# Feed-forward of a decoder layer: two-level matrix products by seven block products in place of eight, layer one then layer two

## The chip, the cores and the metric

The kernel runs on one core of a Trainium2 chip. The metric is the device time of that core in microseconds (us), from launch to end; three runs of the kernel before gave 1788.17, 1789.99 and 1790.69, median 1789.99.

The engines are called PE (matrix products), PEld (its weight loads), DVE (vector), ACT (scalar, activations), POOL (GpSimd) and SP (the queue that issues all loads and stores here).

## The reference

One layer of a decoder with 1024 tokens of width 1024 and a feed-forward width of 4096. Only the last part is touched by the change:

```python
y = jnp.einsum('bsk,kd->bsd', y_mix, w_out)              # output projection
x = layer_norm(DEEPNORM_ALPHA * x + (1.0 + g1) * y, ln1_g, ln1_b)
h = x * (1.0 + sc2) + sh2
ff = jnp.einsum('bsf,fd->bsd',
                jnp.square(jax.nn.relu(jnp.einsum('bsd,df->bsf', h, w_ff_in))),
                w_ff_out)
x = layer_norm(DEEPNORM_ALPHA * x + (1.0 + g2) * ff, ln2_g, ln2_b)
```

Ahead of it stand an input projection, a state-space scan and attention, which the change leaves as they are.

## The kernel before

All data are 32-bit floats. A product of two matrices is made from high and low parts: `hi` is the operand rounded to the matrix engine's format, `lo` the rest, and each product is three matmuls, hi·hi, hi·lo and lo·hi. Making the two parts is called a split here (`split`, lines 79 to 88): one cast for `hi` (ACT or POOL) and one subtraction on DVE for `lo` (line 85), which reads two tiles in SBUF.

The stages are, in order of time: modulation and input projection, scan, attention, then the output projection with the first LayerNorm (a loop over 8 blocks of 128 tokens, `tb`, lines 778 to 798), then the feed-forward (lines 800 to 900).

In the loop over `tb`, `norm` makes the normalized rows `u`, and `to_h2`, one block late, transposes them on PE (line 766, PSUM slots "S"), applies scale and bias on ACT (line 769) and splits the result into `h2` (ACT, DVE).

The feed-forward walks over 32 tiles `f` of 128 of the 4096 hidden columns. `ff1(f)` loads and splits a tile of `w1`, runs 48 matmuls of 512 columns (two token halves, 8 steps of k, 3 parts) and makes relu, square and split of the activations: ACT line 821, POOL line 822, ACT line 823, DVE line 824. `w2_prep(f)` loads a tile of `w2`, multiplies it by the gate row on POOL (line 831) and splits it. The activations never leave SBUF. Tiles are taken in groups (14 of two tiles, then one of four); per group the second layer runs over the 8 token blocks, and each result, 1024 columns in one PSUM slot "S", is added to the block's accumulator `ffacc` by DVE (line 883; ACT line 881 in the first group). POOL adds the residual at some point between (lines 876 to 878). In the last group each block goes straight from its matmuls to the second LayerNorm (`norm`, lines 739 to 748), two more row operations (lines 898, 899) and the store.

The kernel is written against a tile framework: tags name rings of buffers (`SLOTS`), a scheduler orders each engine's instructions, and each engine then runs its own list strictly in order. All DMAs stand in one list, SP's.

Of the kernel before, what the change touches and what calls it, by code (L numbers as in the profile page):

```python
# [32 lines left out]
def layer_kernel(ctx, tc, x, xT, cols, rows3, w_ada, b_ada, w_in, w_dtf, w_out, ln_rows, w1, w2, out):  # L33
# [767 lines left out]
    acctags = ["pt"] * 4 + ["P"] * 3 + ["cum"]  # L801
    acc = [None] * TB
    with after(marks["y", 1, 7]):
        g2row = mod_row(G2, "cum", "g2row")

    def ff1(f):
        with after(marks["y", 1, 7]):
            w, _ = w_prep(w1[f], tag=("w", "P")[f % 2])
        ahi = R4("qk", "a_hi")
        alo = R4("qk", "a_lo")  # L810
        for half in range(2):
            hs = slice(half * 512, half * 512 + 512)
            o = PT(("mm", "t", "o", "t")[(2 * f + half) % 4], "mm_ps")
            for k in range(KT):
                xhi, xlo = (t[:, k % 4, :] for t in h2[half][k // 4])
                whi, wlo = wk_(w, k)
                mm(o, whi, xhi, k == 0, False)
                mm(o, whi, xlo, False, False)
                mm(o, wlo, xhi, False, k == KT - 1)
            r = sm.tile([P, 512], F32, name="ffr", tag="o_half", bufs=2)  # L820
            nc.scalar.activation(r, o, AF.Relu)  # L821
            nc.gpsimd.tensor_tensor(r, r, r, op=ALU.mult)  # L822
            nc.scalar.copy(ahi[:, hs], r)  # L823
            nc.vector.tensor_tensor(alo[:, hs], r, ahi[:, hs].bitcast(F32), op=ALU.subtract)  # L824
        return ahi, alo

    def w2_prep(f, tag):
        raw = T4("raw", "raw_w2")
        with after(marks["y", 1, 7]):
            load(raw, w2[f * P:(f + 1) * P, :])  # L830
        nc.gpsimd.tensor_tensor(raw, raw, g2row, op=ALU.mult)  # L831
        hi = R4(tag, "w2_hi")
        lo = R4(tag, "w2_lo")
        split(raw, hi, lo, "act")
        return hi, lo

    groups = [2] * 14 + [4]
    f = 0
    for gi, gf in enumerate(groups):
        final = gi == len(groups) - 1  # L840
        a = []
        w = []
        for i in range(gf):
            a.append(ff1(f))
            w.append(w2_prep(f, "v" if i < 2 else "misc" if i == 2 else "w"))
            f += 1
        if final:
            with after(marks["y", 1, 7]):
                ln2g = row(2, "hx", "ln2g")
                ln2b = row(3, "hx", "ln2b")  # L850
        for tb in range(TB):
            ts = slice(tb * P, (tb + 1) * P)
            last = final and tb == TB - 1
            if last:
                oh = [PT("S", "s_ps"), PT("S", "s_ps")]
            else:
                o = PT("S", "s_ps", (P, 1024))
                oh = [o[:, :512], o[:, 512:]]
            for half in range(2):
                ds = slice(half * 512, half * 512 + 512)  # L860
                for i in range(gf):
                    mm(oh[half], a[i][0][:, ts], w[i][0][:, ds], i == 0, False)
                    mm(oh[half], a[i][0][:, ts], w[i][1][:, ds], False, False)
                    mm(oh[half], a[i][1][:, ts], w[i][0][:, ds], False, i == gf - 1)
            u = acc[tb]
            if gi == 1 and tb == 0:
                with after(marks["y", 1, 7]):
                    ln1g = row(0, "misc", "ln1g")
                    ln1b = row(1, "misc", "ln1b")
                nc.gpsimd.tensor_scalar(ln1g, ln1g, ALPHA, 1.0, op0=ALU.mult, op1=ALU.mult)  # L870
                nc.gpsimd.tensor_scalar(ln1b, ln1b, ALPHA, 1.0, op0=ALU.mult, op1=ALU.mult)
            if gi == tb + 1:
# [85 lines left out]
```

## Time and profile before

| | |
|---|---|
| median of three runs | 1789.99 us (1788.17 to 1790.69) |
| profiled execution: span | 1789.5 us |
| mean granted PE clock over the span | 0.988 |
| PE busy | 1731.2 us, 97% |
| DVE busy | 1136.4 us, 64% |
| POOL busy | 731.2 us, 41% |
| ACT busy | 607.2 us, 34% |

The profiled execution's span is 1789.5 us; its three timed siblings have their median 0.5 us above that. A busy share is the time in which an engine executes something; PE at 97% has very little time in which it waits. The feed-forward is the stretch from about 1070 us to the end.

### The profile page before, as it was taken

To read this page: it belongs to the slowest core of one execution; us is meant where nothing else is said; L and a number is where in the kernel's file an instruction comes from. 1 tells how busy PE (TensorE), PEld (TensorE's weight loads), DVE (VectorE), ACT (ScalarE), POOL (GpSimd) and SP (SyncE) were. 2 spreads that over 40 slices of the span, in tenths; PEclk is the share of its full clock that TensorE was granted. 3 is DMA by queue.
4 is the path that set the end of the run, shared out by engine and by line. 5 is a ranking of instruction groups with operands and counts; after the bars stand their busy time and mean duration, and the time that the engine had idled before them with its cause. 6 is when DMAs were issued, how large, how long until landed. Compare 5 with 4: busy or idle time off the path is not lost.

```text
span 1789.5 us, 22841 instructions
## 1 busy us (share of the span) xinstructions
PE 1731.2 (97%) x8676; PEld 1441.7 (81%) x8676; DVE 1136.4 (64%) x1771; ACT 607.2 (34%) x1035; POOL 731.2 (41%) x634
## 2 busy tenths in 40 slices
PE   7989999999999999999999999999999999999996
PEld 6768888888888888887788887888888888888885
DVE  7778687768777777757664774354554544455448
ACT  3445333314444545446654443211111111111121
POOL 5143344335445444424423547444444432223235
PEclk9989999999999999999999999999999999999998
DMA  8134334322233232223237442211111111111112
GB/s 322 36 131 132 114 133 138 110 71 82 83 117 102 93 115 89 64 62 127 97 129 235 136 175 102 71 60 59 48 59 59 59 47 48 47 48 47 48 71 94
DMA packets 73117, 172.76 MB, mean 97 GB/s; under 512 B 7696, under 2 KB 34576, under 8 KB 73008
## 3 DMA queue, kind: packets, MB, share of 16 engines
q1 hardware_dynamic: 73008, 171.31, 28.4%
q8 instruction: 68, 1.11, 0.3%
q14 instruction: 41, 0.34, 0.1%
HBM read 140.74 MB, written 22.15 MB: 91 GB/s over the span
## 4 chain that ended last, share of the span: by engine, by line
PE 75%; DVE 12%; DMA 4%; ACT 3%; issue 3%; POOL 3%; SPq 0%; DVEq 0%; POOLq 0%; ACTq 0%
PE mm_ps L62 45%; PE s_ps L62 22%; PE o_ps L62 4%; PE t_ps L523 3%; DVE ada_red L134 2%; DMA raw_ada<-in_w_ada_dram 1%; DVE conv_a L326 1%; DVE scores L398 1%; DVE w_hl L85 1%; DVE scores L396 1%; DVE probs L496 1%; DMA raw_o<-in_w_out_dram 1%; DVE h_hl L85 1%; DVE ffacc L898 0%; DVE pt_hl L526 0%
## 5 line engine op out<-in xcount | busy, mean ns | idle before, releaser
L62 PE MATMUL mm_ps<-h_hl,w_hl 128*128 128x512 f32 x3552 | 865.8, 396 | 6.0 <-DVE w_hl L85 4.6
L62 PEld LDWEIGHTS mm_ps<-h_hl,w_hl 128*128 128x128 f32 x3552 | 660.3, 189 | 142.2 <-DVE w_hl L85 7.0
L883 DVE TENSOR_TENSOR ffacc<-ffacc,s_ps 128x1024 f32<-128x1024 f32 x104 | 126.1, 1220 | 187.5 <-PE s_ps L62 187.5
L85 DVE TENSOR_TENSOR w_hl<-raw_w,w_hl 128x512 fp32r<-128x512 f32 x152 | 141.8, 949 | 99.2 <-POOL w_hl L79 99.0
L62 PE MATMUL s_ps<-w_hi,a_hi 128*128 128x512 f32 x512 | 199.9, 390 | 2.2 <-DVE ffacc L739 2.2
L62 PE MATMUL s_ps<-w_lo,a_hi 128*128 128x512 f32 x512 | 199.8, 390 | 0.0
L62 PE MATMUL s_ps<-w_hi,a_lo 128*128 128x512 f32 x512 | 198.2, 391 | 0.1
L79 POOL TENSOR_SCALAR w_hl<-raw_w 128x512 fp32r<-128x512 f32 x150 | 103.8, 701 | 188.8 <-PE mm_ps L62 85.6
L501 POOL TENSOR_SCALAR probs<-probs,m 128x128 f32<-128x128 f32 (+7 forms) x128 | 102.4, 803 | 155.9 <-DVE m L500 134.8
L822 POOL TENSOR_TENSOR ffr<-ffr 128x512 f32<-128x512 f32 x64 | 80.4, 1257 | 203.4 <-ACT ffr L821 203.3
L132 POOL TENSOR_TENSOR raw_ada<-raw_ada,c_act 128x1024 f32<-128x1024 f32 x44 | 90.1, 2055 | 117.3 <-DMA raw_ada<-in_w_ada_dram 95.9
L499 ACT ACTIVATE probs<-probs,m 128x128 f32<-128x128 f32 (+7 forms) x128 | 99.2, 776 | 91.0 <-DVE m L498 77.3
L821 ACT ACTIVATE ffr<-mm_ps 128x512 f32<-128x512 f32 x64 | 38.2, 597 | 268.6 <-PE mm_ps L62 265.3
L824 DVE TENSOR_TENSOR a_lo<-ffr,a_hi 128x512 fp32r<-128x512 f32 x64 | 65.1, 1017 | 93.2 <-ACT a_hi L823 90.7
L496 DVE CUSTOM_DVE_ANT_0 probs<-s_ps,cumrow 128x128 f32<-128x128 f32 (+7 forms) x128 | 95.1, 753 | 36.3 <-PE s_ps L62 23.0
L62 PEld LDWEIGHTS s_ps<-w_hi,a_hi 128*128 128x128 f32 x512 | 96.5, 189 | 22.8 <-DVE ffacc L739 2.7
L62 PE MATMUL o_ps<-pt_hl,v_s 128*128 128x256 f32 (+1 forms) x640 | 110.6, 294 | 3.6 <-DVE m L498 1.5
L525 ACT CAST pt_hl<-t_ps 128x512 fp32r<-128x512 f32 (+1 forms) x160 | 84.5, 541 | 86.5 <-PE t_ps L523 83.9
L62 PEld LDWEIGHTS s_ps<-w_hi,a_lo 128*128 128x128 f32 x512 | 96.4, 188 | 20.6 <-DVE a_lo L824 0.6
L526 DVE TENSOR_TENSOR pt_hl<-t_ps,pt_hl 128x512 fp32r<-128x512 f32 (+1 forms) x160 | 99.8, 633 | 20.4 <-ACT pt_hl L525 19.1
L62 PEld LDWEIGHTS s_ps<-w_lo,a_hi 128*128 128x128 f32 x512 | 96.5, 188 | 20.1
L831 POOL TENSOR_TENSOR raw_w<-raw_w,g2row 128x1024 f32<-128x1024 f32 x32 | 81.2, 2538 | 70.5 <-DMA raw_w<-in_w_dram 67.4
(209 smaller groups left out, 2557.1 us busy)
## 6 DMA issues: line engine op xcount, KB each, us to landing
raw_w<-in_w_dram SPq DMA_DIRECT2D x64, 512.0 KB, 3.3
raw_ada<-in_w_ada_dram SPq DMA_DIRECT2D x48, 512.0 KB, 3.8
raw_w<-in_w_in_dram SPq DMA_DIRECT2D x44, 512.0 KB, 3.6
arow<-rowd SPq DMA_DIRECT2D x16, 512.0 KB, 4.0
cumrow<-rowd SPq DMA_DIRECT2D x16, 512.0 KB, 3.6
q<-q_st SPq DMA_DIRECT2D x128, 64.0 KB, 2.0
y_raw<-yd SPq DMA_DIRECT2D x16, 512.0 KB, 4.5
raw_o<-in_w_out_dram SPq DMA_DIRECT2D x16, 512.0 KB, 3.4
```

What stands on the lines that cost most here:

```text
L62: nc.tensor.matmul(o, l, r, start=start, stop=stop)
L79: nc.gpsimd.tensor_scalar(hi, raw, 1.0, 1.0, op0=ALU.mult, op1=ALU.mult)
L85: eng.tensor_tensor(lo, raw, hi.bitcast(F32), op=ALU.subtract)
L132: nc.gpsimd.tensor_tensor(raw, raw, c_act.unsqueeze(2).broadcast_to([P, KT, P]), op=ALU.mult)
L496: nc.vector.tensor_tensor_reduce(out=pt, in0=sp[:, :W], in1=cum[:, :W], op0=ALU.add, op1=ALU.max, scale=1.0, scalar=-3.0e38, accum_out=m[: ...
L499: nc.scalar.activation(pt, pt, AF.Exp, bias=m[:, 1:2], scale=1.0, accum_out=m[:, 2:3])
L501: nc.gpsimd.tensor_scalar(pt, pt, m[:, 3:4], 1.0, op0=ALU.mult, op1=ALU.mult)
L525: nc.scalar.copy(hl[:, 0, :n], tp[:, :n])
L526: nc.vector.tensor_tensor(hl[:, 1, :n], tp[:, :n], hl[:, 0, :n].bitcast(F32), op=ALU.subtract)
L822: nc.gpsimd.tensor_tensor(r, r, r, op=ALU.mult)
L831: nc.gpsimd.tensor_tensor(raw, raw, g2row, op=ALU.mult)
L883: nc.vector.tensor_tensor(u, u, o, op=ALU.add)
```

## The change

Both layers of the feed-forward are computed by Strassen's scheme in Winograd's form: each matrix is cut into 2 by 2 blocks, sums and differences of blocks are formed first, seven block products are made in place of eight, and their sums give the four result blocks.

Layer 1 runs first for all hidden columns, in 16 `Pair`s of two `f` tiles. A pair is 7 products of 12 matmuls each (84 in place of 96). The operands on the side of `h2` are seven half-by-half matrices: three (numbers 1, 2, 3) are split in `to_h2`, four (5, 6, 4, 7) need differences between blocks of both token halves and are split by `h_split` behind the last block, as 16 tiles of 512 columns. On the weight side POOL makes four sums of 512 columns per pair, and ACT and DVE split all seven. Results are gathered in four PSUM banks X, Y, Z, V; even pairs take the banks "mm", "o", "t", "t", odd pairs the two slots "S". ACT copies four of them to SBUF, DVE adds three from PSUM and one from SBUF, and makes relu and square in one operation (four per pair, both inputs in SBUF). `out` stores the blocks and, after four more sums on POOL, the sums that layer 2 needs: seven tiles a pair, to DRAM.

Layer 2 covers 28 of the 32 tiles by Strassen, in seven "doubles" (groups of 2, 2, 2 and 1), and the last four tiles by plain products. Each double has seven products of 24 matmuls. Per product and double the activations come back from DRAM (512 KB), and both they and the `w2` sum (POOL) are split again. Each of the seven products has an accumulator `Q` of its own; ACT fills it in the first group, DVE adds to it in the others. In the last group DVE also makes the seven sums of 2048 columns that give the result blocks. POOL then multiplies by the gate row and adds the residual, 32 operations of 512 columns, and the last four tiles, the LayerNorm and the store follow per token block as before. The residual is now prepared during the first groups and kept in DRAM (`resd`).

Matmuls of 512 columns in the feed-forward: 1536 + 1536 before; 16·84 + 7·7·24 + 4·48 = 1344 + 1176 + 192 after.

The core of the diff:

```diff
+        if tb >= 4:
+            b12, b22 = hts
+            for i in range(2):
+                ks = slice(2 * i, 2 * i + 2)
+                t1, t4 = hf[0][:, ks, js], hf[1][:, ks, js]
+                sub(eng, t1, b12[:, ks, :], t1)
+                sub(eng, t3f[i][:, :, js], b22[:, ks, :], b12[:, ks, :])
+                sub(eng, t2f[i][:, :, js], b22[:, ks, :], t1)
+                sub(eng, t4, t4, t2f[i][:, :, js])
...
+    def h_split(o, src, tags):
+        hb_hl[o] = []
+        for k in range(4):
+            t = R4(tags[k], "h2_s", (P, 2, 512))
+            split(src(k), t[:, 0, :], t[:, 1, :], "act")
...
+    def w1_ops(n):
...
+        yield 1, op(a11)
+        yield 2, op(a12)
+        s3 = sm.tile([P, 4, P], F32, name="w_s3", tag="o_half", bufs=2)
+        sub(nc.gpsimd, s3, a11, a21)
+        add(nc.gpsimd, a21, a21, a22)
+        sub(nc.gpsimd, a11, a21, a11)
+        sub(nc.gpsimd, a12, a12, a11)
...
+        def run(self, steps):
...
+            def square(i):
+                nc.vector.scalar_tensor_tensor(c[:, i, :], c[:, i, :], 0.0, c[:, i, :], op0=ALU.max, op1=ALU.mult)
...
+                elif st == 7:
+                    self.product("X", False, True)
+                    nc.scalar.copy(u3, bank["X"])
+                    add(nc.vector, c[:, 1, :], bank["V"], u3)
+                    square(1)
+                    add(nc.vector, c[:, 2, :], p5, u3)
+                    square(2)
...
+    ORDER = (1, 2, 5, 6, 4, 7, 3)
+    first = [Pair(0), Pair(1)]
+    for p in first:
+        p.run(ORDER[:2])
+    h_split(5, lambda k: hf[0][:, k, :], ["qk"] * 4)
...
+    for gi, gd in enumerate(DOUBLES):
...
+                split(src, bhl[0], bhl[1], "act")
+                al_ = T4("v", "a_ld", shape=(P, 2, 512))
+                load(al_, adr[d][AD[i]])
+                ahl = [R4(t, "a_op", (P, 2, 512)) for t in atags]
+                split(al_, ahl[0], ahl[1], "act")
...
+                if gi == 0:
+                    nc.scalar.copy(q, o)
+                else:
+                    add(nc.vector, q, q, o)
+            if last:
+                if i == 2:
+                    add(nc.vector, Q[2], Q[2], Q[1])
...
+                elif i == 5:
+                    add(nc.vector, Q[3], Q[3], Q[6])
+                    add(nc.vector, Q[3], Q[3], Q[5])
+                    add(nc.vector, Q[5], Q[5], Q[7])
...
+        for h, u in enumerate(us):
+            ds = slice(h * 512, h * 512 + 512)
+            nc.gpsimd.tensor_tensor(u, u, g2row[:, ds], op=ALU.mult)
+            add(nc.gpsimd, u, u, rs[:, ds])
```

How the lists of the engines stand around two places. The first is the start of the feed-forward, where the last token block's rows `u` are transposed (`t_ps`). On PE before, the transposes are followed at once by the first layer's matmuls on operands that are already there:

```order
L766 MATMUL t_ps_9846<-identf_69,u1_9741 128x128 [waits Activation_49]
L766 MATMUL t_ps_9846<-identf_69,u1_9741 128x128 x3
L62 MATMUL mm_ps_9951<-h2_hl_8990,w_hl_9943 128x512 [waits Pool_49]
L62 MATMUL mm_ps_9951<-h2_hl_8991,w_hl_9943 128x512
L62 MATMUL mm_ps_9951<-h2_hl_8990,w_hl_9943 128x512 [waits DVE_49]
```

On PE now, one product of such operands (`h2_hl_8990`) is left, and behind it stands product 5 of the first pair, whose operands `h2_s_9997` and `w_op_10050` are made after the transposes; the matmuls on `h2_hl_8992` stand in the list behind that:

```order
L787 MATMUL t_ps_9880<-identf_69,u1_9769 128x128 x3
L911 MATMUL f_ps_9918<-h2_hl_8990,w_op_9964 128x512 [waits Activation_49]
L911 MATMUL f_ps_9918<-h2_hl_8990,w_op_9964 128x512 x5
L911 MATMUL f_ps_9918<-h2_hl_8991,w_op_9964 128x512 x6
L911 MATMUL f_ps_9913<-h2_s_9997,w_op_10050 128x512 [waits Activation_49]
L911 MATMUL f_ps_9913<-h2_s_9997,w_op_10050 128x512 [waits DVE_49]
...
L911 MATMUL f_ps_9914<-h2_s_10030,w_op_10082 128x512
L911 MATMUL f_ps_9918<-h2_hl_8992,w_op_9980 128x512 [waits Activation_49]
```

On ACT at the same place, these are the rows ahead of the cast of `w_op_10050` (the last eleven of 20 casts that stand between the last transposed block's activations and it):

```order
L81 CAST h2_s_10009<-h2_t2_8998 128x512 [waits DVE_49]
L81 CAST h2_s_10012<-h2_t2_8998 128x512
L81 CAST h2_s_10039<-h2_t3_9001 128x512 [waits DVE_49]
L81 CAST h2_s_10042<-h2_t3_9001 128x512
L81 CAST h2_s_10015<-h2_t2_8999 128x512 [waits DVE_49]
L81 CAST h2_s_10018<-h2_t2_8999 128x512
L81 CAST h2_s_10021<-h2_f_8997 128x512 [waits DVE_49,Pool_49]
L81 CAST h2_s_10024<-h2_f_8997 128x512
L81 CAST w_op_10082<-raw_w_9925 128x512 [waits DMAHW5_49]
L81 CAST h2_s_10027<-h2_f_8997 128x512 [waits DVE_49,Pool_49]
L81 CAST h2_s_10030<-h2_f_8997 128x512
L81 CAST w_op_10050<-raw_w_9925 128x512 [waits Pool_49]
```

Before, ACT had two casts there (`h2_hl_8994`, `h2_hl_8996`) and one of a weight.

The second place is the last group of layer 2. On DVE before, rows of this kind, one for each 12 matmuls of 512 columns, stood ahead of the last group, and the last group's own blocks went to the LayerNorm:

```order
L883 TENSOR_TENSOR ffacc_10106<-ffacc_10106,s_ps_13600 128x1024 [waits DVE_49,PE_49]
L824 TENSOR_TENSOR a_lo_13651<-ffr_13707,a_hi_13650 128x512 [waits Activation_49]
L883 TENSOR_TENSOR ffacc_10121<-ffacc_10121,s_ps_13614 128x1024 [waits DVE_49,PE_49]
L883 TENSOR_TENSOR ffacc_10136<-ffacc_10136,s_ps_13628 128x1024 [waits DVE_49,PE_49]
L85 TENSOR_TENSOR w2_lo_13716<-raw_w2_13712,w2_hi_13715 128x1024 [waits DVE_49,Activation_49]
```

On DVE now, the end of the last group (`q_acc_12387` is Q2, `12314` Q3, `12466` Q6, `12539` Q7, `12612` Q5, `12687` Q4); a row of 2048 columns is a sum of two accumulators, and those of one accumulator and `s_ps` free a PSUM slot:

```order
L765 TENSOR_TENSOR q_acc_12539<-q_acc_12539,q_acc_12466 128x2048 [waits DVE_49]
L765 TENSOR_TENSOR q_acc_12612<-q_acc_12612,s_ps_14066 128x1024 [waits PE_49]
L765 TENSOR_TENSOR q_acc_12612<-q_acc_12612,s_ps_14080 128x1024 [waits PE_49]
L85 TENSOR_TENSOR a_op_14166<-a_ld_14163,a_op_14165 128x1024 [waits DMAHW3_49,Activation_49]
L85 TENSOR_TENSOR w2_op_14173<-raw_w2_14169,w2_op_14172 128x1024 [waits Activation_49]
L765 TENSOR_TENSOR q_acc_12314<-q_acc_12314,q_acc_12612 128x2048 [waits DVE_49]
L765 TENSOR_TENSOR q_acc_12687<-q_acc_12687,s_ps_14108 128x1024 [waits PE_49]
L765 TENSOR_TENSOR q_acc_12612<-q_acc_12612,q_acc_12539 128x2048 [waits DVE_49]
L765 TENSOR_TENSOR q_acc_12687<-q_acc_12687,s_ps_14122 128x1024 [waits PE_49]
L85 TENSOR_TENSOR a_op_14179<-a_ld_14176,a_op_14178 128x1024 [waits DMAHW5_49,Activation_49]
L765 TENSOR_TENSOR q_acc_12687<-q_acc_12687,q_acc_12539 128x2048 [waits DVE_49]
L85 TENSOR_TENSOR w2_op_14186<-raw_w2_14182,w2_op_14185 128x1024 [waits Activation_49]
```

On POOL now, ahead of the first power of the last LayerNorm (`mv_14264`, which in the kernel before stood directly behind the last activations' squares):

```order
L765 TENSOR_TENSOR q_acc_12314<-q_acc_12314,res_14207 128x512 [waits Pool_49]
L1116 TENSOR_TENSOR q_acc_12687<-q_acc_12687,g2row_13843 128x512 [waits DVE_49,PE_49]
L1116 TENSOR_TENSOR q_acc_12687<-q_acc_12687,g2row_13843 128x512 x3
L765 TENSOR_TENSOR q_acc_12612<-q_acc_12612,res_14213 128x512 [waits DMAHW0_49,Pool_49]
L765 TENSOR_TENSOR q_acc_12612<-q_acc_12612,res_14219 128x512 [waits DMAHW4_49,Pool_49]
L765 TENSOR_TENSOR q_acc_12612<-q_acc_12612,res_14225 128x512 [waits DMAHW6_49,Pool_49]
L765 TENSOR_TENSOR q_acc_12612<-q_acc_12612,res_14231 128x512 [waits DMAHW7_49,Pool_49]
L1106 TENSOR_TENSOR mv_14264<-mv_14264,mhalf_87 128x1 [waits DVE_49]
```

So 28 of the 32 gate and residual operations stand ahead of that power; the other four follow it.

## Rows read from the trace of the kernel before

**Rows 1.** Page, part 1: busy time and share by engine.

```profile
PE 1731.2 (97%) x8676; PEld 1441.7 (81%) x8676; DVE 1136.4 (64%) x1771; ACT 607.2 (34%) x1035; POOL 731.2 (41%) x634
```

**Rows 2.** Windows: us, PE, PEld, DVE, ACT, POOL busy (count), PEclk, DMA share, GB/s.

```profile
1000.00:1100.00 100.00, 96.31 (x453) 79.52 (x453) 73.20 (x95) 44.39 (x95) 56.04 (x48) 0.98 0.47 163
1200.00:1300.00 100.00, 100.00 (x443) 82.81 (x442) 48.32 (x41) 14.98 (x22) 42.89 (x28) 1.00 0.17 56
1700.00:1790.00 90.00, 75.23 (x324) 61.46 (x322) 59.51 (x88) 18.67 (x22) 40.34 (x34) 0.93 0.22 82
```

**Rows 3.** Waits of PE from 1020 us on: total, times, longest.

```profile
PE t_ps L766 <- DVE u L750: 3.7, 1, 3.7
PE s_ps L62 <- DVE ffacc L739: 2.2, 1, 2.2
```

**Rows 4.** Timeline of PE, start of the feed-forward: start, duration, work, count, idle before.

```profile
1068.75 0.39 PE L62 MATMUL mm_ps<-wo_hi,y_hl 128*128 128x512 f32 x1
...
1069.77 5.73 PE L62 MATMUL mm_ps<-h_hl,w_hl 128*128 128x512 f32 x24
1079.18 1.06 PE L766 MATMUL t_ps<-identf,u 128*128 128x128 f32 x8 [3.69 <-DVE u L750]
```

**Rows 5.** Windows behind the two waits, columns as in Rows 2.

```profile
1080.00:1085.00 5.00, 5.00 (x18) 3.70 (x17) 2.52 (x4) 4.72 (x11) 0.10 (x1) 0.66 0.60 211
1770.00:1775.00 5.00, 2.77 (x9) 1.90 (x8) 4.30 (x9) 1.24 (x1) 2.52 (x3) 0.83 0.28 105
```

**Rows 6.** Groups on ACT from 1020 us on: busy, mean ns, idle before.

```profile
L81 ACT CAST w_hi<-raw_w 128x1024 fp32r<-128x1024 f32 x32 | 32.6, 1053 | 116.3 <-PE s_ps L62 105.5 <-POOL raw_w L831 10.8
L769 ACT ACTIVATE h_t<-t_ps,b2t,g2t 128x128 f32<-128x128 f32 x48 | 17.8, 461 | 25.8 <-PE t_ps L766 25.8
...
L81 ACT CAST h_hl<-h_t 128x512 fp32r<-128x512 f32 x12 | 7.3, 635 | 0.3
```

**Rows 7.** Groups on DVE from 1020 us on.

```profile
L883 DVE TENSOR_TENSOR ffacc<-ffacc,s_ps 128x1024 f32<-128x1024 f32 x104 | 126.1, 1220 | 187.5 <-PE s_ps L62 187.5
...
L85 DVE TENSOR_TENSOR w_lo<-raw_w,w_hi 128x1024 fp32r<-128x1024 f32 x32 | 48.5, 1551 | 13.4 <-ACT w_hi L81 13.4
...
L739 DVE TENSOR_TENSOR ffacc<-ffacc,s_ps 128x512 f32<-128x512 f32 x16 | 10.3, 680 | 2.6 <-PE s_ps L62 2.6
...
L85 DVE TENSOR_TENSOR h_hl<-h_t,h_hl 128x512 fp32r<-128x512 f32 x12 | 8.0, 678 | 0.0
```

**Rows 8.** Groups on POOL from 1020 us on.

```profile
L831 POOL TENSOR_TENSOR raw_w<-raw_w,g2row 128x1024 f32<-128x1024 f32 x32 | 81.2, 2538 | 70.5 <-DMA raw_w<-in_w_dram 67.4 <-DVE w_hl L85 3.0
L822 POOL TENSOR_TENSOR ffr<-ffr 128x512 f32<-128x512 f32 x64 | 80.4, 1257 | 203.4 <-ACT ffr L821 203.3
```

**Rows 9.** Timelines of DVE, then POOL: the same DVE operation alone and beside POOL.

```profile
1083.72 1.23 DVE L85 TENSOR_TENSOR w_lo<-raw_w,w_hi 128x1024 fp32r<-128x1024 f32 x1 [2.48 <-ACT w_hi L81]
...
1092.11 3.32 DVE L85 TENSOR_TENSOR w_lo<-raw_w,w_hi 128x1024 fp32r<-128x1024 f32 x1 [5.96 <-ACT w_hi L81]
...
1091.95 2.40 POOL L877 TENSOR_TENSOR x<-x,ln1b 128x1024 f32<-128x1024 f32 x1
```

**Rows 10.** Window of a stretch in which DVE and POOL are both full.

```profile
1092.00:1104.00 12.00, 11.86 (x52) 9.50 (x52) 10.78 (x6) 3.69 (x7) 12.00 (x7) 1.00 0.25 87
```

**Rows 11.** Timeline at 1300 us: a DVE add from PSUM beside POOL.

```profile
1301.37 2.40 POOL L876 TENSOR_TENSOR x<-x,ln1g 128x1024 f32<-128x1024 f32 x1 [3.69 <-DMA x<-x2d]
...
1302.37 1.22 DVE L883 TENSOR_TENSOR ffacc<-ffacc,s_ps 128x1024 f32<-128x1024 f32 x1 [4.45 <-PE s_ps L62]
```

**Rows 12.** Timeline of the last stage: two successive blocks on DVE, the last matmul.

```profile
1753.43 1.28 DVE L739 TENSOR_TENSOR ffacc<-ffacc,s_ps 128x512 f32<-128x512 f32 x2
...
1759.46 1.28 DVE L739 TENSOR_TENSOR ffacc<-ffacc,s_ps 128x512 f32<-128x512 f32 x2
...
1777.06 0.40 PE L62 MATMUL s_ps<-w_hi,a_lo 128*128 128x512 f32 x1
```

More of the change, by code (lines that the diff above doesn't have):

```diff
@@ L766, in to_h2 @@
                 nc.tensor.transpose(tp[:, b * P:(b + 1) * P], u[:, k * P:(k + 1) * P], identf)
+            if tb < 4:
+                ht = hf[hb][:, :, js]
+            else:
+                ht = sm.tile([P, 4, P], F32, name="h2_t", tag="o_half", bufs=2)
             for b in range(4):
@@ L798, in layer_kernel @@
     to_h2(*before)
[L801 to L847, printed above, removed]
-            with after(marks["y", 1, 7]):
[L849 to L853, printed above, removed]
-            if last:
[L855 to L872, printed above, removed]
@@ new lines, in layer_kernel @@
+    ORDER = (1, 2, 5, 6, 4, 7, 3)
[3 more added lines that the diff above has]
+    h_split(5, lambda k: hf[0][:, k, :], ["qk"] * 4)
+    h_split(6, lambda k: t2f[k // 2][:, k % 2, :], ["qk"] * 4)
+    h_split(4, lambda k: hf[1][:, k, :], ["v", "v", "w", "w"])
+    h_split(7, lambda k: t3f[k // 2][:, k % 2, :], ["pt"] * 4)
+    for p in first:
+        p.run(ORDER[2:])
+    for n in range(2, NP):
+        Pair(n).run(ORDER)
+    AD = {1: 0, 2: 1, 4: 2, 5: 3, 6: 4, 7: 5, 3: 6}
@@ new lines, in layer_kernel, with w2_double @@
+    wtags = ["raw", "raw", "cum", "cum", "ex", "ex", "ex", "w", "w", "w"]
+    wn = [0]
+    w2r = w2.rearrange("(n i p) d -> p i n d", i=2, p=P)
+    def w2_double(d):
+        r = {}
+        for key, i, h in ((11, 0, 0), (22, 1, 1), (21, 1, 0), (12, 0, 1)):
+            t = T4(wtags[wn[0] % len(wtags)], "raw_w2", shape=(P, 2, 512))
+            wn[0] += 1
+            with after(marks["y", 1, 7]):
+                load(t, w2r[:, i, 2 * d:2 * d + 2, h * 512:h * 512 + 512])
+            r[key] = t
+        return r
@@ new lines, in layer_kernel @@
+                store(resd[tb], x2)
+        if gi == 2:
+            with after(marks["y", 1, 7]):
+                g2row = mod_row(G2, "misc", "g2row")
+                ln2g = row(2, "misc", "ln2g")
+                ln2b = row(3, "misc", "ln2b")
+    fa, fw = [], []
+    for i in range(4):
+        al_ = T4("v", "a_ld")
+        load(al_, adl[i])
+        ahl = [R4(t, "a_op") for t in atags]
+        split(al_, ahl[0], ahl[1], "act")
+        fa.append(ahl)
+        f = 2 * NS + i
+        rw = T4(wtags[i], "raw_w2")
+        with after(marks["y", 1, 7]):
+            load(rw, w2[f * P:(f + 1) * P, :])
+        nc.gpsimd.tensor_tensor(rw, rw, g2row, op=ALU.mult)
+        whl = [R4("qk", "w2_op") for _ in range(2)]
+        split(rw, whl[0], whl[1], "act")
+        fw.append(whl)
@@ new lines, in norm2 @@
+    def norm2(us, oh):
+        st = sm.tile([P, 2, 6], F32, name="bn", tag="bn", bufs=2)
+        mv = sm.tile([P, 4], F32, name="mv", tag="mv", bufs=2)
+        for i in range(2):
+            add(nc.vector, us[i], us[i], oh[i])
+            nc.vector.bn_stats(st[:, i, :], us[i])
+        nc.vector.bn_aggr(mv[:, 0:2], st)
+        nc.vector.tensor_scalar(mv[:, 2:3], mv[:, 1:2], LN_EPS, None, op0=ALU.add)
+        nc.gpsimd.tensor_tensor(mv[:, 3:4], mv[:, 2:3], mhalf[:, 0:1], op=ALU.pow)
+        return mv
@@ L944 @@
     from concourse.bass_utils import run_bass_kernel_spmd
[L946 removed]
+    nc = bacc.Bacc("TRN2", target_bir_lowering=False, num_devices=1, dynamic_dma_scratch_size=1024)
     laid = prepare(inputs)
```

222 lines of the change are left out of this document (192 added, 30 removed).

## Prediction

> **What bounds the kernel now.** I read the page's busy shares first, then windows by stage, then the waits of PE. PE is busy 97% of the span, the next engine, DVE, 64% [rows 1]. Between 1200 and 1300 us PE is busy 100.00 us of 100 with 443 matmuls at granted clock 1.00; DVE is busy 48, POOL 43, ACT 15 [rows 2]. So the feed-forward is bound by the number of matmuls, one per 100/443 = 0.2257 us, and everything else hides under it. From 1020 us to the end PE waits twice only: 3.7 us for the last block's normalized rows and 2.2 us for a DVE add near the end [rows 3]. What lies off PE is the tail: the last matmul starts at 1777.06 [rows 12], ends 0.4 later, and the span is 1789.5, so 12.0 us.
>
> **What the change removes.** 3072 matmuls of 512 columns become 2712: 360 fewer. At 0.2257 us that is **-81.3 us**, if PE stays as full as in [rows 2]. PE's lead came from slack on the others; the change spends that slack, so the rest of the sum is the idle time that it brings to PE, stage by stage.
>
> **Start of layer 1.** The last old matmul starts at 1068.75, the transposes of the last block at 1079.18, after 24 filling matmuls and 3.69 us of idle [rows 4]. After the change two products of 12 fill the same hole, so that wait stays. Behind the transposes PE now has one ready product (12 x 0.2257 = 2.7 us) and is out of work at 1079.2 + 1.0 + 2.7 = 1082.9. The next row needs the cast of w_op_10050, ahead of which ACT has 8 activations at 0.461 (3.7 us) and 20 casts, 18 of 512 columns at 0.635 and two of 256, which I take at half, in all some 12.1 us [rows 6]: 1079.4 + 15.8 = 1095.2, that is 12.3 us of idle. The low part on DVE comes later: 8 differences of 256 columns and some 19 subtractions of 512 at 0.678 [rows 7] make 15.6 us clean from about 1081, and POOL makes eight weight sums of 512 (8 x 1.257 = 10.1 us [rows 8]) that collide with them (below): 1097 to 1107. I take 12 us of idle. After a wait of 3.7 us the clock fell to 0.66 for 5 us [rows 5], and 9 matmuls behind the 2.23 us wait took some 0.43 us each, nearly double (the stretch 1770 to 1775 at 0.83 [rows 5]): 9 x 0.2 = 1.8 us for such a fall. Together **+14** (10 to 24).
>
> **LayerNorm loop.** For blocks 4 to 6 POOL gets eight differences of 256 columns (8 x 0.65 = 5.2 us, half of the 512 row [rows 8]) in a stretch where it is at 56% and DVE at 73% [rows 2]. The power that `norm` waits for stands behind them. **+2** (0 to 5).
>
> **The shared resource of DVE and POOL.** A subtraction of 1024 columns with two SBUF inputs takes 1.23 us alone and 3.32 us when a POOL operation of 2.40 us has begun just before [rows 9]: about the sum of the two. An add from PSUM inside a POOL operation keeps its 1.22 us [rows 11]. So two-SBUF operations on DVE and POOL operations take turns. Over a longer stretch the turns are not strict: in the 12 us of [rows 10] DVE's six operations and POOL's seven have clean durations of some 4.7 and 9.2 us (from [rows 7 to 9]), 13.9 in all, so a factor of 0.87 on a sum turn by turn. The Trainium skill has a rule for this in SBUF — State Buffer (section "SBUF: two separate sides"): the port pair of the two engines is an exclusive lock for a whole instruction, taken by whichever starts first, and the other blocks; operands in PSUM stay out of it. The trace agrees with it in the 3.32 and the 1.22 us and not in the 0.87; by the rule the sums below are those called turn by turn, and it speaks against this change, which adds just such operations.
>
> **Layer 1, steady.** A pair takes PE 84 x 0.2257 = 18.96 us. DVE has 12 two-SBUF operations of 512 (seven low parts, four squares, one add), 12 x 0.678 = 8.1 us, and three PSUM adds (2.0 us). POOL has eight of 512, 10.1 us. Turn by turn 8.1 + 10.1 = 18.2 us, 96% of PE's time; at the factor of [rows 10] 15.8, 84%. ACT has 11 operations near 0.62, under 7 us. Loads and stores are some 2.8 MB per pair, 148 GB/s, below the 163 GB/s that ran beside a PE of 96% [rows 2]. PE's list mixes two pairs, so a late operand holds it only when both are late. It fits, narrowly: I take 0.3 us a pair, **+5** (0 to 24; the upper end is 1.5 us a pair).
>
> **Layer 1 to layer 2.** The first split of stored activations needs buffers and PSUM slots that the last pair frees: one copy, one cast and one subtraction of 1024 in a row (1.05 + 1.05 + 1.23, [rows 6, 9]), **+3.5** (0 to 8).
>
> **Layer 2, groups of two.** A step (one product of both doubles) takes PE 48 x 0.2257 = 10.8 us. DVE has four subtractions of 1024 (4.9 us) and two PSUM adds of 1.22; POOL has 8 sums of 1024 in 7 steps (2.9 us a step at 2.538) and in some eight of the 21 steps the residual (two of 1024, 5.1 us): 7.8 us turn by turn, 12.9 with the residual, 11.2 at the factor. **+4** (0 to 11).
>
> **Last group.** One double: PE needs only 168 x 0.2257 = 37.9 us, and 5.4 for the first block of the plain products: 43.3. DVE has 14 subtractions (17.2), 14 adds (17.1), seven sums of 2048 (twice 1.23, 17.2) and eight subtractions for the plain tiles (9.8): 61 us clean, in its list ahead of the first LayerNorm add. POOL's 28 operations of 512 ahead of the first power (35 us) fall into the same stretch. DVE becomes the bound: first block at 62 in place of 43, **+19** (10 to 28), and one more clock fall, **+2** (0 to 4).
>
> **Final blocks.** From then on DVE's pitch sets the end, 6.03 us a block (1753.43 to 1759.46 [rows 12]) against PE's 24 x 0.2257 = 5.42: 7 x 0.6 = **+4** (0 to 12). The tail of 12.0 stays.
>
> **Sum.** 14 + 2 + 5 + 3.5 + 4 + 19 + 2 + 4 = 53.5 of idle against 81.3 removed: 1789.5 - 27.8 = 1761.7 for the profiled execution; the median of the runs is 0.5 above, so **1762 us**, 1.6% faster. All lower ends together (20) give 1728, all upper ends (116) 1825.
>
> **Rivals.** (a) *The stalls are mostly hidden*: 20 to 35 us of idle, 1728 to 1744. For it: PE's list mixes products of two pairs, and DVE and POOL have slack of half in the feed-forward today [rows 2]. Against: at the start of layer 1 and in the last group the counts of ACT and DVE alone exceed PE's, whatever the order. Chance 0.20.
> (b) *The turns of DVE and POOL bound layer 1* (the other side): each pair takes what DVE and POOL need one after the other, with gaps where one waits for ACT. The whole of DVE and POOL in a row is 8.1 + 2.0 + 10.1 = 20.2 us, 1.3 above PE: 16 x 1.3 = 21 in place of 5, 1778. It decides from 21 us a pair on: (21.0 - 18.96) x 16 = 33 in place of 5 gives 1790; at 23 us it would be 1822. For it: 96% where the turns are strict; against: the 0.87 of [rows 10]. The Trainium skill's rule above (SBUF — State Buffer) is the strict case. Chance of reaching beyond 1780: 0.22, of which 0.16 beyond 1793 and 0.04 within the measurement of 1790.
> (c) *The clock stays low through the last group*, because PE is busy 38 us of 62 in pieces: 168 matmuls at 0.43 us are 72 us in place of 61, +11 and a like slowing of the plain products' start, some 1775. For it: one wait of 2.2 us was enough in [rows 5]; against: each time it was back within some 5 us. Chance 0.10.
> My forecast, 1744 to 1780 by its own terms without (c): 0.48.
>
> **Numbers.** A measurement here can tell about 0.2% (3.6 us) from no change. Faster: 0.20 + 0.48 + 0.10 + 0.02 of (b) = 0.80; same 0.04; slower 0.16. The range leaves a tenth on each side: the lower third of (a), and the part of (b) beyond 21.4 us a pair: 1735 to 1796. The forecast's own range is 1744 to 1780.
>
> **What would show it.** Windows over layer 1: 442 or 443 matmuls per 100 us and PE near 98% if the pairs fit, under 92% if (b) holds (18.96/20.6), with DVE's 512 low parts well above 0.678 us. In the waits of PE, one of 10 us or more at product 5 of the first pair, released by ACT or DVE; in the last group several for PSUM slots released by DVE adds, with the mean clock of that stretch under 1.00. DVE busy nearly throughout the last group. The prediction is wrong if PE waits little in the last group (DVE's sums moved off the path), or if the waits stand evenly over all pairs or all steps of layer 2.

## The result and the profile after

Four runs of the changed kernel have a median of 1779.60 us (1777.44 to 1781.84), four of the kernel before 1790.33: a ratio of 0.9945, 95% interval 0.9931 to 0.9959 (the two medians alone give 0.9940, inside it). The change is faster by 0.55%, clear of what a measurement can tell, and a third of the 1.6% that was forecast. The profiled execution has a span of 1775.7 us, 13.8 below that of before; it is the fastest of its four, and each run's time is 1.7 us above its span. The page's busy shares of it, which answer to [rows 1]:

```profile
PE 1664.6 (94%) x8316; PEld 1378.7 (78%) x8316; DVE 1335.7 (75%) x1934; ACT 714.3 (40%) x1194; POOL 874.3 (49%) x674
```

The 360 matmuls are gone (8676 to 8316), and PE's share falls from 97% to 94%: what was saved on PE comes back mostly as time in which PE waits. Windows over the feed-forward, columns as in [rows 2]:

```profile
1080.00:1100.00 20.00, 7.80 (x20) 5.17 (x18) 17.87 (x21) 15.58 (x33) 14.87 (x14) 0.59 0.06 22
1110.00:1390.00 280.00, 280.00 (x1237) 231.94 (x1236) 200.99 (x221) 92.05 (x162) 173.79 (x113) 1.00 0.43 149
1400.00:1420.00 20.00, 14.83 (x56) 11.08 (x55) 13.98 (x12) 8.11 (x9) 11.15 (x5) 0.91 1.02 393
1500.00:1520.00 20.00, 18.08 (x74) 14.48 (x73) 20.00 (x10) 4.77 (x5) 20.00 (x7) 0.91 0.37 131
1680.00:1700.00 20.00, 11.24 (x40) 8.58 (x39) 20.00 (x12) 3.98 (x4) 10.26 (x5) 0.83 0.00 0
1720.00:1740.00 20.00, 14.95 (x59) 11.92 (x58) 12.29 (x16) 1.52 (x2) 18.54 (x17) 0.83 0.00 1
```

In layer 1, from 1110 to 1390 us, PE is busy 280.00 of 280 us: no pair costs anything. The loss stands at four places: the start of layer 1 (20 matmuls in 20 us, where 88 fit), the step to layer 2, a stretch around 1510 where DVE and POOL are both at 20.00 of 20, and the last group. The waits of PE from 980 us on, in place of the two of [rows 3]:

```profile
PE s_ps L62 <- DVE q_acc L765: 24.7, 12, 5.5
PE f_ps L911 <- DVE h_s L85: 7.4, 1, 7.4
PE f_ps L911 <- ACT w_op L81: 6.4, 1, 6.4
PE t_ps L787 <- ACT h_hl L81: 5.4, 1, 5.4
PE s_ps L62 <- DVE w_op L85: 4.5, 2, 3.8
PE s_ps L62 <- ACT f_e L939: 3.7, 1, 3.7
...
```

The start of layer 1 on PE (start, duration, work, count, idle before), which answers to [rows 4]:

```profile
1079.05 1.94 PE L787 MATMUL t_ps<-identf,u 128*128 128x128 f32 x8 [5.36 <-ACT h_hl L81]
1083.49 5.16 PE L911 MATMUL f_ps<-h_hl,w_op 128*128 128x512 f32 x12 [2.50 <-ACT h_t L794]
1095.09 1.65 PE L911 MATMUL f_ps<-h_s,w_op 128*128 128x512 f32 x3 [6.44 <-ACT w_op L81]
1104.13 0.80 PE L911 MATMUL f_ps<-h_s,w_op 128*128 128x512 f32 x1 [7.39 <-DVE h_s L85]
```

PE stands most of the time from 1073 to 1104, and behind the first two waits its clock is at the lower of its two levels: the twelve matmuls from 1083.49 take 5.16 us, where 2.7 do at the upper one. ACT's cast comes where the forecast had it (1095), but the matmul behind waits for a low part from DVE, nine microseconds on. Between 1066.7 and 1125.1 PE made 120 matmuls and 20 transposes, 29.2 us of work in 58.4, so 29.2 us are lost; the same place lost 5.8 before.

The last group, first DVE, then POOL, then PE:

```profile
1715.23 0.15 DVE L1105 TENSOR_SCALAR mv<-mv 128x1 f32<-128x1 f32 x1
...
1731.92 3.67 DVE L1131 SCALAR_TENSOR_TENSOR mv<-mv 128x1 f32<-128x1 f32 x1 [4.65 <-POOL mv L1106]
...
1726.36 5.02 POOL L765 TENSOR_TENSOR q_acc<-q_acc,res 128x512 f32<-128x512 f32 x4
1731.34 0.55 POOL L1106 TENSOR_TENSOR mv<-mv,mhalf 128x1 f32<-128x1 f32 x1
1731.86 3.69 POOL L765 TENSOR_TENSOR q_acc<-q_acc,res 128x512 f32<-128x512 f32 x3
...
1694.82 9.80 PE L62 MATMUL s_ps<-w_op,a_op 128*128 128x512 f32 x33 [5.48 <-DVE q_acc L765]
...
1736.24 13.27 PE L62 MATMUL s_ps<-w_op,a_op 128*128 128x512 f32 x48 [5.05 <-DVE q_acc L765]
```

DVE has the first block's variance ready at 1715.4, but POOL makes its power only at 1731.34, behind 28 gate and residual operations, and DVE stands 4.65 us in front of the step that needs it. That step, on one scalar per partition, then stretches to 3.67 us, as long as POOL's next three operations. In the kernel before, the same step of a block in the same stage was:

```profile
1753.35 0.16 DVE L747 SCALAR_TENSOR_TENSOR mv<-mv 128x1 f32<-128x1 f32 x1 [0.66 <-POOL mv L743]
```

PE waits for the PSUM slot behind it. From 1635.73 to 1763.14 PE made 398 matmuls, 89.8 us of work in 127.4.

### The profile page after: what moved, and what is told of

The parts are those of the page before. It is cut to its first block, busy times and chain, and to the rows that moved or that the text cites. A ratio compares the mean times of both kernels' runs of the same rounds, so it can differ in the third digit from the quotient of the medians.

```text
span 1775.7 us, 22866 instructions
## 1 busy us (share of the span) xinstructions
PE 1664.6 (94%) x8316; PEld 1378.7 (78%) x8316; DVE 1335.7 (75%) x1934; ACT 714.3 (40%) x1194; POOL 874.3 (49%) x674
## 4 chain that ended last, share of the span: by engine, by line
PE 67%; DVE 16%; issue 5%; POOL 4%; DMA 4%; ACT 3%; SPq 0%; DVEq 0%; POOLq 0%; ACTq 0%
PE mm_ps L62 26%; PE s_ps L62 17%; PE f_ps L911 17%; PE o_ps L62 3%; PE t_ps L523 3%; DVE ada_red L134 2%; DMA raw_ada<-in_w_ada_dram 2%; DVE q_acc L765 2%; DVE w_hl L85 1%; DVE conv_a L326 1%; DVE scores L398 1%; DVE probs L496 1%; POOL q_acc L1116 1%; DVE scores L396 1%; DVE a_op L85 1%
## 5 line engine op out<-in xcount | busy, mean ns | idle before, releaser
L62 PE MATMUL mm_ps<-h_hl,w_hl 128*128 128x512 f32 x2016 | 502.1, 399 | 6.9 <-DVE w_hl L85 4.5
L62 PEld LDWEIGHTS mm_ps<-h_hl,w_hl 128*128 128x128 f32 x2016 | 369.9, 189 | 82.8 <-DVE w_hl L85 6.7
L62 PE MATMUL s_ps<-w_op,a_op 128*128 128x512 f32 x1368 | 324.0, 398 | 34.4 <-DVE q_acc L765 24.7
L62 PEld LDWEIGHTS s_ps<-w_op,a_op 128*128 128x128 f32 x1368 | 261.6, 192 | 96.5 <-issue 12.9
L85 DVE TENSOR_TENSOR w_op<-raw_w,w_op 128x512 fp32r<-128x512 f32 (+1 forms) x149 | 191.5, 1293 | 46.8 <-ACT w_op L81 46.3
L81 ACT CAST w_op<-raw_w 128x512 fp32r<-128x512 f32 (+1 forms) x149 | 114.1, 775 | 213.6 <-PE s_ps L62 110.7
L911 PE MATMUL f_ps<-h_s,w_op 128*128 128x512 f32 x768 | 184.1, 393 | 14.9 <-DVE h_s L85 7.4
L911 PEld LDWEIGHTS f_ps<-h_s,w_op 128*128 128x128 f32 x768 | 145.5, 190 | 47.1 <-DVE h_s L85 8.1
L911 PE MATMUL f_ps<-h_hl,w_op 128*128 128x512 f32 x576 | 141.4, 396 | 2.5 <-ACT h_t L794 2.5
L911 PEld LDWEIGHTS f_ps<-h_hl,w_op 128*128 128x128 f32 x576 | 110.3, 192 | 26.1 <-ACT h_t L794 2.9
```

Source lines behind the costliest of these rows:

```text
L62: nc.tensor.matmul(o, l, r, start=start, stop=stop)
L81: nc.scalar.copy(hi, raw)
L85: eng.tensor_tensor(lo, raw, hi.bitcast(F32), op=ALU.subtract)
L911: nc.tensor.matmul(o, l, r, start=first and k == 0 and m == 0, stop=last and k == 3 and m == 2, skip_group_check=True)
```

## Experiments

Ratios are to the kernel before on the same chip; the changed kernel has 0.9945, and a ratio 0.001 lower is 1.8 us less.

**e1: POOL's prework behind the powers.**

```diff
...
+        if tb < 4:
+            with after(power[tb]):
+                scale_add(tb + 4)
```

> Edit: POOL's gate and residual operations for token blocks 4 to 7 are ordered behind the powers of blocks 0 to 3; nothing else is changed. Theory A (POOL's list ahead of the first power holds the last LayerNorms, and DVE and PE behind them): the DVE wait of 4.65 us for POOL at 1732 and the PE wait of 5.05 us at 1736 go, 1772 to 1775 us in place of 1779.6. Theory B (DVE's own list sets the end, and the moved operations only collide with DVE later): 1778 to 1781.

Measured: 0.9923 (0.9907 to 0.9940), some 4 us less than the changed kernel. The intervals overlap; with e7 it holds. POOL's order is a cost, at the lower end of what A expected.

**e2: a group of one first.**

```diff
-    DOUBLES = (2, 2, 2, 1)
+    DOUBLES = (1, 2, 2, 2)
```

> Edit: the doubles are taken in groups of 1, 2, 2, 2 in place of 2, 2, 2, 1. Theory A (in the last group DVE has the seven sums and 22 splits over only 43 us of PE work): PE now has 81 us of matmuls over some 78 us of DVE, the idle time of the last group falls by 8 to 14 us, 1766 to 1772. Theory B (POOL's 32 operations and the port that they share with DVE set the end, however long the group is): under 4 us, 1776 to 1780.

Measured: 0.9912 (0.9897 to 0.9927), 6 us less, between A and B. PE's waits from 1630 us on fall from 26.6 to 14.7, and the first group, now of one, gives some back at the step between the layers (5.8 us there for a copy on ACT). More PE work over the last sums helps, and does not settle it.

**e3: split, then its products.**

```diff
     h_split(5, lambda k: hf[0][:, k, :], ["qk"] * 4)
+    for p in first:
+        p.run((5,))
     h_split(6, lambda k: t2f[k // 2][:, k % 2, :], ["qk"] * 4)
...
```

> Edit: each of the four late operands of layer 1 is split and used by both first pairs before the next is split, so that PE's list has product 5 of pair 0 whole and ahead of product 4. Theory A (the order of the lists: PE stands at a matmul whose operand is the last but few that DVE makes): the wait of 7.39 us at 1104 goes in part, 4 to 7 us, 1773 to 1776. Theory B (DVE's subtractions themselves, stretched by POOL's weight sums through the shared port, are late, in any order): 0 to 2 us, 1777 to 1780.

Measured: 0.9950 (0.9933 to 0.9966), nothing. PE's list now has product 5 first, but the scheduler left DVE's list nearly as it was; the wait moved to the low part of the weights, 10.4 us for DVE. A fell as it was put here: the order that counts is DVE's.

**e4: no prework.**

> Edit: leaves out the 32 POOL operations of gate and residual ahead of the last LayerNorm (the output lacks both), and their loads. Theory A (those operations take the port from DVE in the last group and stand ahead of the powers): the end comes 14 to 20 us earlier, 1760 to 1766, and DVE's sums of 2048 columns take 2.3 us each. Theory B (DVE alone is the bound there, 61 us against 43): 5 to 9 us, 1771 to 1775.

Measured: 0.9851 (0.9836 to 0.9866), 17 us less. The four costliest groups of DVE from 1630 us on (busy, mean ns), the changed kernel:

```profile
L85 DVE TENSOR_TENSOR w_op<-raw_w,w_op 128x1024 fp32r<-128x1024 f32 x12 | 23.3, 1938 | 0.0
L765 DVE TENSOR_TENSOR q_acc<-q_acc,s_ps 128x1024 f32<-128x1024 f32 x18 | 21.5, 1210 | 3.6 <-PE s_ps L62 3.6
L85 DVE TENSOR_TENSOR a_op<-a_ld,a_op 128x1024 fp32r<-128x1024 f32 x12 | 20.5, 1708 | 0.0
L765 DVE TENSOR_TENSOR q_acc<-q_acc 128x2048 f32<-128x2048 f32 x7 | 18.4, 2631 | 0.0
```

and without the prework:

```profile
L85 DVE TENSOR_TENSOR a_op<-a_ld,a_op 128x1024 fp32r<-128x1024 f32 x13 | 22.3, 1712 | 0.0
L765 DVE TENSOR_TENSOR q_acc<-q_acc,s_ps 128x1024 f32<-128x1024 f32 x18 | 21.5, 1214 | 3.7 <-PE s_ps L62 3.7
L85 DVE TENSOR_TENSOR w_op<-raw_w,w_op 128x1024 fp32r<-128x1024 f32 x12 | 17.8, 1487 | 0.6 <-ACT w_op L81 0.6
L765 DVE TENSOR_TENSOR q_acc<-q_acc 128x2048 f32<-128x2048 f32 x7 | 16.0, 2286 | 0.0
```

The adds from PSUM keep their 1.21 us in both. Of the operations with two SBUF inputs, the splits of the weights (23.3 to 17.8) and the sums (18.4 to 16.0) get shorter; the splits of the activations keep a mean of 1.71 us, because most of their long ones run before 1652 us, beside weight sums on POOL that both kernels have. These 8 us of DVE's time are about half of the gain. The rest fits the powers, which no longer stand behind the prework: the first one starts at 1710.81 in place of 1731.34. The loads left out with the prework are no rival, since the DMA share of the changed kernel from 1680 to 1740 us is 0.16 at most. A holds.

**e5: late splits ordered behind.**

```diff
+    first[0].run((5,))
+    with after(w_lo[-1]):
+        h_split(6, lambda k: t2f[k // 2][:, k % 2, :], ["qk"] * 4)
+    first[0].run((6,))
+    first[1].run((5, 6))
+    with after(w_lo[-1]):
+        h_split(4, lambda k: hf[1][:, k, :], ["v", "v", "w", "w"])
...
```

> Edit: at the start of layer 1 the splits of operands 6, 4 and 7 are ordered behind the low part of product 5's weights, so that DVE makes only what product 5 needs ahead of it. Theory A (order: product 5 stands behind subtractions that it does not need): its first matmuls run by 1096 in place of 1104, 5 to 8 us of idle less, a ratio to the kernel before of 0.990 to 0.992 in place of 0.9945. Theory B (DVE and POOL are late with all of it, and what product 5 gains product 6 or 4 loses): 0.9935 to 0.995.

Measured: 0.9904 (0.9887 to 0.9922), 7 us less. PE:

```profile
1090.23 0.82 PE L912 MATMUL f_ps<-h_s,w_op 128*128 128x512 f32 x2 [3.51 <-ACT w_op L81]
1091.70 4.63 PE L912 MATMUL f_ps<-h_s,w_op 128*128 128x512 f32 x10 [0.64 <-DVE w_op L85]
```

**e6: no weight sums for the first two pairs.**

> Edit: leaves out the eight weight sums on POOL of the first two pairs (their products take the unsummed weights); the order is that of the changed kernel. Theory A (the shared port: POOL's sums stretch DVE's subtractions between 1086 and 1102): DVE's six subtractions take 0.7 us each in place of 1.33, product 5 runs on 6 to 9 us earlier, ratio 0.989 to 0.991. Theory B (order of the lists, or ACT's 20 casts): 0 to 2 us, 0.9935 to 0.995.

Measured: 0.9888 (0.9870 to 0.9906), 10 us less. The same six subtractions on DVE, in the changed kernel and then here:

```profile
1095.49 7.97 DVE L85 TENSOR_TENSOR h_s<-h_t,h_s 128x512 fp32r<-128x512 f32 x6
```

```profile
1092.72 3.69 DVE L85 TENSOR_TENSOR h_s<-h_t,h_s 128x512 fp32r<-128x512 f32 x6
```

So 7.97 us are 3.69 without POOL's sums, and PE, which in the changed kernel went on at 1104.1, goes on at 1096.6. Both A theories, of e5 and of e6, hold: PE waits because POOL stretches DVE operations that stand ahead of the one needed.

**e7: e1 and e2 together; e8: and blocks 4 to 7 on DVE.**

> Edit: the two edits of the last group together (prework behind the powers, groups 1, 2, 2, 2). Theory A (two separate costs: POOL's list and too little PE work in the last group): their gains add, ratio near 0.989. Theory B (both end at one limit, the port of DVE and POOL): no better than 0.991.

> Edit: as e7, and the gate and residual operations of token blocks 4 to 7 run on DVE in place of POOL. Theory A (POOL's time and the port are the limit at the end: 16 operations of 1.25 us on POOL against 16 of 0.65 us on DVE): 4 to 8 us less than e7. Theory B (DVE's own time is the limit there): 0 to 6 us more than e7.

Measured: e7 0.9876 (0.9860 to 0.9891), 12 us less: the gains add, A. In its trace DVE waits 0.66 us for the first power, in place of 4.65:

```profile
1714.57 1.23 DVE L1139 SCALAR_TENSOR_TENSOR mv<-mv 128x1 f32<-128x1 f32 x1 [0.66 <-POOL mv L1106]
```

e8 0.9894 (0.9879 to 0.9910): nothing gained over e7, rather 3 us lost (the intervals overlap), B; DVE has no time to give in the last stage.

**e9: casts behind the copy.**

```diff
+                if gi == 0 and step < 2:
+                    with after(pair.u3):
+                        split(al_, ahl[0], ahl[1], "act")
...
```

> Edit: at the step from layer 1 to layer 2 the first casts of stored activations on ACT are ordered behind the last pair's copy of u3 (in the changed kernel ACT waits for their loads ahead of that copy, and PE for the copy, 3.74 us at 1404.7). Theory A (ACT's list): 2 to 4 us less, ratio 0.992 to 0.9935. Theory B (the loads, at some 400 GB/s with the DMA engines full from 1396 on, are late anyway, and PE waits for the operands instead): 0.994 to 0.9955.

Measured: 0.9931 (0.9911 to 0.9952): 2.5 us, less than its interval. ACT of the changed kernel shows what stood there:

```profile
1403.12 1.04 ACT L81 CAST a_op<-a_ld 128x1024 fp32r<-128x1024 f32 x1 [0.21 <-DMA a_ld<-ad]
1404.07 0.58 ACT L939 COPY f_e<-f_ps 128x512 f32<-128x512 f32 x1
```

The copy that frees PE's slot stands behind casts that wait for loads. The wait of 3.74 us is gone in e9, and in its place PE waits four times, 5.9 us in all: twice for PSUM banks that DVE empties (2.8) and twice for operands (3.1). Inconclusive in time, near B in the rows.

**e10: e5, e7 and e9 together.**

> Edit: the edits that gained, together: late splits ordered behind, prework behind the powers, groups 1, 2, 2, 2, and the casts behind the copy. Theory A (separate idle stretches at three places, which add): 7 + 12 us and 0 to 3 for the last, ratio 0.982 to 0.985. Theory B (what is gained at one place is given back later, since DVE and POOL are full through the feed-forward): no better than 0.987.

Measured: 0.9855 (0.9836 to 0.9875), median 1764.01 us, 16 us less than the changed kernel, where the single gains add to 20 to 22. It beats both kernels. The bounds of A and B lie inside or at the edge of the interval, so how much is given back stays open. Its trace shows one place: at the step between the layers 11.4 us are lost (60 matmuls in 25.0 us from 1388.20), more than the 8.6 of the changed kernel. On ACT another cast stands ahead of a copy there, one that waits for a weight sum on POOL; e2 and e7 have the like, with a wait of 5.8 us on PE, and e9's edit does not move it:

```profile
1398.07 1.05 ACT L81 CAST w_op<-raw_w 128x1024 fp32r<-128x1024 f32 x1 [5.21 <-POOL raw_w L768]
1399.02 0.58 ACT L935 COPY f_e<-f_ps 128x512 f32<-128x512 f32 x1
```

**e11: no block sums.**

> Edit: leaves out the seven sums of 2048 columns of the last group (the output blocks are then wrong), on the changed kernel. Theory A (DVE's time is what the last group lacks, 18 us of it these sums): 12 to 18 us less, ratio 0.985 to 0.988. Theory B (POOL's 32 operations and their place in POOL's list set the end): under 6 us, 0.991 to 0.9945.

Measured: 0.9823 (0.9801 to 0.9846), 22 us less, more than A's 18. The sums' own time on DVE is 18.4 us; without them POOL's prework on the blocks also starts earlier, which this run does not separate. With e4: DVE's time and POOL's turns both lie on the path there.

**e12: sums twice in layer 1.**

> Edit: POOL makes each of the four activation sums of a pair twice in layer 1 (14 pairs, 5 us more of POOL per pair). Theory A (layer 1 stands close to the limit of the port that DVE and POOL take in turns: 8.1 + 15.1 = 23.2 us turn by turn against 18.96 of PE): 17 to 60 us more, ratio 1.004 to 1.028. Theory B (room enough, PE stays full): under 5 us more, 0.9945 to 0.9975.

Measured: 1.0128 (1.0112 to 1.0144), 33 us more, A. The window of layer 1:

```profile
1110.00:1390.00 280.00, 258.20 (x1103) 209.40 (x1102) 220.50 (x198) 81.34 (x145) 231.94 (x151) 0.97 0.37 129
```

1103 matmuls in 280 us are 21.3 us a pair, in place of 18.96: 0.92 of the 23.2 us turn by turn. With four POOL operations more in each pair, what rival (b) of the prediction describes is there. Not all of it need be turns, though. DVE's adds from PSUM, which had waited 3.8 us for POOL in the same window of the changed kernel, wait 28.4 us for its doubled sums here, and the run does not separate the order of POOL's list from the turns:

```profile
L765 DVE TENSOR_TENSOR a_c<-f_ps,f_e 128x512 f32<-128x512 f32 x38 | 25.8, 684 | 36.8 <-POOL a_s L768 28.4 <-PE f_ps L911 4.2 <-ACT f_e L939 4.2
```

**e13 and e14: spare matmuls in PE's waits.**

```diff
+    def spare(n, o, ins):
+        x = hop(1, 0)[0]
+        with after(ins):
+            for _ in range(n):
+                nc.tensor.matmul(o, x[:, :128], x, start=True, stop=True, skip_group_check=True)
...
```

> Edit: on the kernel of e3 (ratio 0.995), 64 spare matmuls of 512 columns on ready operands are put where PE waits at the start of layer 1, into banks that are overwritten later; they add nothing to the result. Theory A (the low clock behind the waits is a price of its own, some 5 us of the 23 lost there): with PE kept going the granted clock of 1080 to 1120 is near 1.00 in place of 0.59 and 0.79, and the time falls by 3 to 6 us, ratio 0.9915 to 0.9935. Theory B (the slow matmuls stand ahead of further waits for DVE and only shorten these): within 2 us of e3, 0.994 to 0.996.

> Edit: on the changed kernel, 8 spare matmuls of 512 columns behind each of the last ten PSUM slots of the last group, into a bank that nothing uses there. Theory A (the clock at 0.83 to 0.91 in the last group costs some 9 us by itself): the clock stays near 1.00 and the time falls by 4 to 9 us, ratio 0.9895 to 0.9925. Theory B (DVE and POOL set the pace there, and a slow matmul only fills PE's waits): within 2 us, or a little more where the spare matmuls stand in the way, 0.9935 to 0.997.

Measured: 0.9950 (0.9932 to 0.9968) and 0.9949 (0.9935 to 0.9964), nothing in either. The window of e13, then that of e14:

```profile
1080.00:1100.00 20.00, 20.00 (x84) 16.45 (x83) 19.31 (x27) 14.42 (x31) 15.03 (x9) 0.94 0.00 0
```

```profile
1680.00:1700.00 20.00, 20.00 (x90) 16.57 (x89) 20.00 (x13) 4.01 (x4) 10.46 (x4) 1.00 0.00 0
```

The granted clock of these windows goes from 0.59 (e3 has 0.59 too) to 0.94 and from 0.83 to 1.00, and the time stays. In e14 it rises only in part of the last group: from 1700 to 1720 it is 0.84, where the changed kernel has 0.91. B: at these places DVE sets the pace, and a slow matmul mostly fills a wait that is there anyway. The intervals leave room for a price of up to some 4 us.

## Why the prediction was right in direction and too large

The mechanism and the places were right: the waits stand at the start of layer 1, where product 5 waits, and in the last group, where PE waits for DVE's adds, and the pairs fit. What failed is the size of two terms.

**Removed work.** 360 matmuls, right by count; layer 1's full window has 0.2263 us for one (1237 in 280 us), against 0.2257. 81.3 us stands.

**Start of layer 1: the first step that failed.** The text bounded the wait by ACT (1095.2) and by DVE (1097 to 1107) and then wrote "I take 12 us of idle", which is ACT's bound, although the matmul waits for both. PE went on at 1104.1, inside the bound that was not taken. The term was +14 and measures 29.2 - 5.8 = 23, near the upper end of its own range, 10 to 24. e6 shows what makes the difference, the 8 POOL sums beside DVE's subtractions, and e5 that the order of DVE's list decides how much of it PE sees.

**Last group and final blocks: the second.** The 61 us on DVE were "clean": the text noted that POOL's 35 us "fall into the same stretch" and added nothing for it. The splits took 1.82 us on average (24 in 43.8) in place of 1.23, the sums 2.63 in place of 2.46. The terms +19, +2 and +4 were 25; measured are 127.4 - 89.8 = 37.6 us, less the 4.0 us that this stage lost before, 34. Counted by matmuls, 1.5 us are lost ahead of the group, and 23.7 up to the end of its first block (192 matmuls in 67.0 us from 1645.82), where 19 + 2 were forecast. Behind it 12.4 are lost (168 matmuls in 50.3 us), 8.4 more than before, where +4 was forecast: the text had POOL's 28 operations ahead of the first power and priced only DVE's pitch. e4 and e1 show POOL's part (e1's 4 us are of that size), e11 DVE's.

**Smaller terms.** The step between the layers, +3.5 (0 to 8), measures 8.6 (79 matmuls in 26.4 us from 1387.81): besides the chain of copy, cast and subtraction there were loads behind a full DMA, which no term had. Layer 1, +5, measures 0. Groups of two, +4: 4.4, around 1510 us, where the residual runs beside the splits. LayerNorm loop, +2: its last matmul starts at 1066.47, 2.3 us earlier than in the one trace of before; the traces of the other runs have it 0.6 to 4.1 us earlier, so no cost of this loop shows. In all 23 + 34 + 8.6 + 4.4 - 2 = 68 in place of 53.5, so 1789.5 - 81.3 + 68 = 1776, and 1775.7 was the span. Both large terms came out high together, since POOL's operations stretch DVE's in both; the sum of middle values took them as if each could fall either way. That layer 1 and the LayerNorm loop came out 9 us under their terms was luck, and hid a part of this. The other 4 us of the miss are the runs: their median is 3.9 above this profiled span, where 0.5 was assumed.

**The rivals.** (a) was out, by the counts of ACT and DVE as argued. (b) did not happen, but e12 shows that the margin was under 5 us of POOL a pair. (c), a low clock through the last group, is in the windows (0.83, [rows 5] has the like) and yet does not set the time: DVE's 18 adds from PSUM wait only 3.6 us in all for PE (the row in e4), and e13 and e14 raise the clock, e14 in part, and gain nothing that shows. The 1.8 and 2 us for a clock fall in the sum are less than these runs can tell.

**The rule on the port.** Turns of DVE and POOL are the common cause of the two large terms. Around 1516 us of the changed kernel, DVE, then POOL:

```profile
1516.51 3.41 DVE L85 TENSOR_TENSOR w_op<-raw_w,w_op 128x1024 fp32r<-128x1024 f32 x1
1519.85 3.41 DVE L85 TENSOR_TENSOR a_op<-a_ld,a_op 128x1024 fp32r<-128x1024 f32 x1
...
1515.47 3.37 POOL L768 TENSOR_TENSOR raw_w<-raw_w,raw_w 128x1024 f32<-128x1024 f32 x1
1518.80 3.37 POOL L1073 TENSOR_TENSOR x<-x,ln1b 128x1024 f32<-128x1024 f32 x1
```

They alternate, one of each every 3.35 us, which is 0.93 of 1.21 + 2.40; e12's pair gives 0.92, with the waits said there. The Trainium skill's rule (SBUF — State Buffer, section "SBUF: two separate sides") has an exclusive lock, held for a whole instruction. These rows agree with it to within 8%, closer than the 0.87 that the prediction took from [rows 10]. The turns are not always one of each: the scalar step at 1731.92 lasted through three operations of POOL.

## What to carry to other kernels

Fewer matmuls pay only where the engines that feed PE have time left, so add up what DVE and POOL do in turns, not each alone, at the places where PE has no other work: starts, steps between stages, ends. Where a matmul waits for two engines, take the later one, stretched by what runs beside it. A low granted clock behind a wait may be only a symptom: see whether the time falls when PE is kept going.

## What the runs showed of the hardware that was not expected

The DMA engines were full for a stretch of 20 us at the step between the layers (share 1.02, 393 GB/s), and loads of 512 KB, which the page of before lands in 3.3 to 4.5 us at the median, took 8.0 (activations) and 8.8 (weights) between 1380 and 1440 us. A low clock cost nothing that shows where a wait for DVE follows: 64 spare matmuls in e13 and 80 in e14 changed the clock and not the time. A step of DVE that takes 0.16 us took 3.67 beside three POOL operations in a row.
